# Down projection of an MLP by Strassen's seven products on two token blocks

## The chip, the cores and the metric

The kernel runs on one core of a Trainium2 chip. The metric is the device time of one execution in microseconds; the median of several runs is compared.

## The reference

One layer of a streaming encoder for 384 tokens, 256 of a new stream and 128 of eight running ones. A mixer (pooling branch, Mamba-2 branch, gates) comes first, then the MLP, which is what the change touches. Width 2048, hidden width 8192, all in float32:

```python
def layer(x, st_pool, st_conv, st_ssm, pos0, p):
    m, new_pool, new_conv, new_ssm = mixer(rmsnorm(x, p['g_mix_pre']), ...)
    x = x + rmsnorm(m, p['g_mix_post'])
    hdn = jnp.square(jax.nn.relu(rmsnorm(x, p['g_mlp_pre']) @ p['w_up'])) @ p['w_down']
    x = x + rmsnorm(hdn, p['g_mlp_post'])
    return x, new_pool, new_conv, new_ssm
```

## The kernel before

The 384 tokens are three blocks of 128. Every matrix product is made of three matmuls on split operands: each float32 operand is cut into a high part (`fp32r`, cast by ScalarE, line 71) and a low part (the rest, by VectorE, line 73), and high x high, high x low and low x high are accumulated in PSUM. Weights come from DRAM as tiles of 128 x 1024 through SyncE's queue (`wfetch`, line 61), are split by `wsplit` (line 66) and rotate through three buffers each for the raw tile, its high and its low part. PSUM is two pools of four banks, `mmtile` and `sstile`.

The mixer takes about the first 1800 us. Then comes the MLP, lines 730 to 803. `x1` (the residual, 3 x 2048 per partition) is transposed and split into `x1h`, `x1l`, the moving operands of the up projection (lines 718 to 727), and its norm factor `r2` is computed beside it. The loop over `c8` takes eight chunks of 1024 hidden rows. In each chunk:

- Up: eight tiles `f8` of 128 hidden rows, each 2 weight tiles x 8 k x 3 matmuls with 384 moving columns (the tokens). The result is scaled, rectified, squared (`ht`), and split into `hh` and `hl`, which have the hidden rows on the partitions.
- Down: four blocks `nb` of 512 output columns. For each, `moving` (line 638) walks four weight tiles of two k each; for each k and each token block `b` three matmuls (lines 648 to 650) with the tokens stationary and 512 weight columns moving. After the last k, VectorE adds the PSUM tile into `hacc` in SBUF (line 778; in the first chunk ScalarE copies it, line 776).

After the last chunk's blocks come the square sums, the gain `gpo2`, the norm and the residual, and the output is stored (lines 781 to 795). A scheduler sets the order of instructions on each engine. The lines that matter in the loop:

```python
for c8 in range(NC):
    hh = []
    for f8 in range(8):
        ...
        hh.append((h, l))
    for nb in range(4):
        o = [mmtile(f"wd{c8}_{nb}_{b}") for b in range(3)]
        ...
        moving(o, [(io["w_down"][c8, nb, kp], ...) for kp in range(4)], hh, ..., done)
```

Of the kernel before, what the change touches and what calls it, by code (L numbers as in the profile page):

```python
# [14 lines left out]
P = 128  # L15
T = 384
TP = 256
NB = 8
TS_ = 16
DM = 2048  # L20
# [14 lines left out]
def build(ctx, tc, io):  # L35
    nc = tc.nc
    v, s, te, gp, sy = nc.vector, nc.scalar, nc.tensor, nc.gpsimd, nc.sync
# [5 lines left out]
    dram = ctx.enter_context(tc.tile_pool(name="dram", bufs=1, space=DRAM))  # L43
# [6 lines left out]
    def mmtile(name):  # L50
        return psm.tile([P, 512], F32, tag="mm", name=name)
# [4 lines left out]
    hold = [None, None]  # L56
# [19 lines left out]
    def wload(src, name):  # L76
        return wsplit(wfetch(src, name))
# [94 lines left out]
    w = wpool.tile([P, 1024], F32, tag="w", name="w_p0_0")  # L172
# [465 lines left out]
    x1 = res.tile([P, 3, DM], F32, name="x1")  # L638
    r2 = res.tile([P, T], F32, name="r2")

    def moving(o, units, lhs, tail, done):
        nk = len(lhs)

        def mm(b, wh, wl, k, k2):
            t = slice(b * P, b * P + P)
            c = slice(k2 * 512, k2 * 512 + 512)
            mh, ml = lhs[k][0][:, t], lhs[k][1][:, t]
            te.matmul(o[b], mh, wh[:, c], start=k == 0, stop=False)  # L648
            te.matmul(o[b], mh, wl[:, c], start=False, stop=False)  # L649
            te.matmul(o[b], ml, wh[:, c], start=False, stop=k == nk - 1)  # L650

        n = len(units)
        for kp in range(n - tail):
            wh, wl = wload(*units[kp])
            for k2 in range(2):
                for b in range(3):
                    mm(b, wh, wl, kp * 2 + k2, k2)
        w = [wload(*units[kp]) for kp in range(n - tail, n)]
        for b in range(3):
            for i, (wh, wl) in enumerate(w):  # L660
                for k2 in range(2):
                    mm(b, wh, wl, (n - tail + i) * 2 + k2, k2)
            done(b)
# [19 lines left out]
    with tc.tile_pool(name="phf", bufs=1, side="right", reuse_waits="tile") as pf, tc.tile_pool(  # L683
# [5 lines left out]
        for nb in range(4):  # L689
# [13 lines left out]
        for i in range(4):  # L703
# [9 lines left out]
                )  # L713
            if i == 0:
                gate[1] = ins
    pga = ctx.enter_context(tc.tile_pool(name="pga", bufs=1, reuse_waits="tile"))
    xs2 = []
    for k in range(KD):
        tr = sstile(f"trm{k}")
# [5 lines left out]
        s.activation(h, tr[:, :T], AF.Copy, scale=g1)  # L725
        v.scalar_tensor_tensor(out=l, in0=tr[:, :T], scalar=g1, in1=h.bitcast(F32), op0=ALU.mult, op1=ALU.subtract)
        xs2.append((h, l))
    mpool.close()

    with tc.tile_pool(name="phg", bufs=1, reuse_waits="tile") as pg, tc.tile_pool(  # L730
        name="phg2", bufs=2, reuse_waits="tile"
    ) as pg2:
        st = pg.tile([P, 3, 4], F32, name="st2")
        for b in range(3):
            for i in range(4):
                q = pg2.tile([P, 512], F32, tag="q3", name=f"q2_{b}_{i}")
                s.activation(q, x1[:, b, blk(i)], AF.Square, accum_out=st[:, b, i : i + 1])
        dg = pg.tile([P, 3, P], F32, name="dg2")
        for b in range(3):
            y = postnorm(pg2, st, b, "n2")  # L740
# [4 lines left out]
        hacc = pg.tile([P, 3, DM], F32, name="hacc")  # L745
        gpo = pg.tile([P, DM], F32, name="gpo2")
        gp.dma_start(gpo, io["g_mlp_post"].partition_broadcast(P))
        st3 = pg.tile([P, 3, 4], F32, name="st3")
        NC = 8
        for c8 in range(NC):  # L750
            hh = []
            for f8 in range(8):
                f = c8 * 8 + f8
                if f == 0:
                    ps = mmtile("pj_up0")[:, :T]
                    half(ps, 0, wload(io["w_up"][0, 0], "up0_0"), xs2)
                    hold[:] = gate
                    half(ps, 1, wload(io["w_up"][0, 1], "up0_1"), xs2)
                else:
                    ps = proj([io["w_up"][f, 0], io["w_up"][f, 1]], xs2, f"up{f}")  # L760
                    hold[:] = [None, None]
                t = pg2.tile([P, T], F32, tag="t", name=f"ht{f}")
                v.scalar_tensor_tensor(out=t, in0=ps, scalar=0.0, in1=r2, op0=ALU.max, op1=ALU.mult)
                s.activation(t, t, AF.Square)
                h = pg2.tile([P, T], F32R, tag=f"hh{f8}", name=f"hh{f}", bufs=1)
                l = pg2.tile([P, T], F32R, tag=f"hl{f8}", name=f"hl{f}", bufs=1)
                s.activation(h, t, AF.Copy)
                v.tensor_tensor(l, t, h.bitcast(F32), ALU.subtract)
                hh.append((h, l))
            for nb in range(4):  # L770
                o = [mmtile(f"wd{c8}_{nb}_{b}") for b in range(3)]

                def done(b):
                    dst = hacc[:, b, blk(nb)]
                    if c8 == 0:
                        s.copy(dst, o[b])
                        return
                    v.tensor_tensor(dst, o[b], dst, ALU.add)
                    if c8 < NC - 1:
                        return  # L780
                    q = pg2.tile([P, 512], F32, tag="q3", name=f"q3_{nb}_{b}")
                    s.activation(q, dst, AF.Square, accum_out=st3[:, b, nb : nb + 1])
                    v.tensor_tensor(dst, dst, gpo[:, blk(nb)], ALU.mult)
                    if nb < 3:
                        return
                    y = postnorm(pg2, st3, b, "n3")
                    for i in range(4):
                        z = hacc[:, b, blk(i)]
                        xb = x1[:, b, blk(i)]
                        if i >= (0, 2, 3)[b]:  # L790
                            s.activation(z, z, AF.Copy, scale=y)
                            gp.tensor_tensor(z, z, xb, ALU.add)
                        else:
                            v.scalar_tensor_tensor(out=z, in0=z, scalar=y, in1=xb, op0=ALU.mult, op1=ALU.add)
                        sy.dma_start(io["y"][b][:, blk(i)], z)

                moving(
                    o,
                    [(io["w_down"][c8, nb, kp], f"wd{c8}_{nb}_{kp}") for kp in range(4)],
                    hh,  # L800
                    3 if c8 == NC - 1 and nb == 3 else 0,
                    done,
                )


def _consts(np):
# [29 lines left out]
def _moving(np, w):  # L836
    r, c = w.shape
    return np.ascontiguousarray(w.reshape(r // 256, 2, P, c // 512, 512).transpose(3, 0, 2, 1, 4)).reshape(c // 512, r // 256, P, 1024)


# [79 lines left out]
```

## Time and profile before

| | |
|---|---|
| Median of 3 runs | 2888.16 us (2887.67 to 2889.95) |
| Span of the profiled execution | 2886.1 us |
| TensorE busy | 2862.9 us (99%) |
| VectorE busy | 1548.9 us (54%) |
| ScalarE busy | 1108.4 us (38%) |
| GpSimd busy | 142.4 us (5%) |
| Moved by the DMA engines | 448.82 MB, 156 GB/s on the mean |

The profile is of one execution, whose own time is not listed beside its span; the three timed runs lie 1.6 to 3.9 us above the span, the median 2.1. PE is TensorE's matmuls, PEld its weight loads, DVE VectorE, ACT ScalarE, POOL GpSimd, SP SyncE. A group of instructions is a line such as "L650 PE MATMUL wd<-wh_wd,hl 128*128 128x512 f32 x768 | 298.9, 389 | 0.0": line 650, engine, operation, output and inputs, shape, count; then busy time in us, the mean of one in ns, and the idle time before them in us with what ended it. In a timeline the first number is the start and the second the duration, in us, and what stands in brackets is the idle time before. A window's row has for each engine its busy time and count in that stretch, then the granted TensorE clock (1 is full speed), the mean busy share of the 16 DMA engines, and GB/s. The rows of DMA issues give the size of one and the median time from issue to landing; queue q1 carries what SyncE issues, q0 what GpSimd issues.

### The profile page before, as it was taken

Reading aid. Unit: us, or ns where it says so; the run is one execution under the profiler, and the core shown is the slowest. Engines: PE = TensorE matmul, PEld = TensorE weight load, DVE = VectorE, ACT = ScalarE, POOL = GpSimd, SP = SyncE. Lnnn points to the kernel's source line nnn. Section 1 sums busy time; section 2 is a strip of 40 time slices with the busy share of each in tenths; the row PEclk is TensorE's granted clock in tenths of the full one; section 3 lists DMA queues with packets and bytes.
Section 4 is the critical chain, followed back from the end, with each engine's and each line's share of the span. In section 5 each row is a group of like instructions: output and inputs, shape, how many; then the busy total and the mean of one; then the engine's idle time right before and its main releaser. Section 6 shows DMA issues by size and latency. Waiting matters only on the chain.

```text
span 2886.1 us, 40192 instructions
## 1 busy us (share of the span) xinstructions
PE 2862.9 (99%) x16165; PEld 2702.5 (94%) x16165; DVE 1548.9 (54%) x2306; ACT 1108.4 (38%) x1628; POOL 142.4 (5%) x178
## 2 busy tenths in 40 slices
PE   9999999999999999999999999999999999999998
PEld 8999999999999999999999988989898998989896
DVE  7773335668678678677533334534444444444445
ACT  5343224445445345344422223533232333333233
POOL 0000000011011011011000000000000000000001
PEclk9999999999999999999999999999999999999999
DMA  6444445466456456466744453434443444444443
GB/s 214 132 130 140 137 137 190 149 200 211 160 196 211 151 203 210 146 221 204 224 147 152 146 179 120 130 126 130 126 130 126 130 126 131 125 131 124 131 125 117
DMA packets 141914, 448.82 MB, mean 156 GB/s; under 512 B 17456, under 2 KB 41072, under 8 KB 137120
## 3 DMA queue, kind: packets, MB, share of 16 engines
q1 hardware_dynamic: 133152, 410.14, 44.9%
q0 software_dynamic: 8576, 36.13, 3.3%
q8 instruction: 126, 2.06, 0.3%
q14 instruction: 60, 0.49, 0.1%
HBM read 404.48 MB, written 41.72 MB: 155 GB/s over the span
## 4 chain that ended last, share of the span: by engine, by line
PE 98%; DVE 1%; DMA 0%; ACT 0%; issue 0%; SPq 0%; DVEq 0%; ACTq 0%
PE pj_up L82 6%; PE pj_up L81 6%; PE pj_up L80 6%; PE wd L650 6%; PE wd L649 6%; PE wd L648 6%; PE pj_x L82 5%; PE pj_x L80 5%; PE pj_x L81 5%; PE pj_z L81 3%; PE pj_z L82 3%; PE pj_z L80 3%; PE pj_sp L80 3%; PE pj_sp L82 3%; PE pj_sp L81 3%; PE pj_gb L80 2%
## 5 line engine op out<-in xcount | busy, mean ns | idle before, releaser
L81 PE MATMUL pj_up<-x1l,wh_up 128*128 128x384 f32 x1024 | 343.2, 335 | 0.0
L80 PE MATMUL pj_up<-x1h,wh_up 128*128 128x384 f32 x1024 | 343.1, 335 | 0.0
L82 PE MATMUL pj_up<-x1h,wl_up 128*128 128x384 f32 x1024 | 342.7, 335 | 0.0
L650 PE MATMUL wd<-wh_wd,hl 128*128 128x512 f32 x768 | 298.9, 389 | 0.0
L649 PE MATMUL wd<-wl_wd,hh 128*128 128x512 f32 x768 | 298.9, 389 | 0.0
L648 PE MATMUL wd<-wh_wd,hh 128*128 128x512 f32 x768 | 298.7, 389 | 0.0
L73 DVE TENSOR_TENSOR wl_wd<-w_wd,wh_wd 128x1024 fp32r<-128x1024 f32 x128 | 156.9, 1225 | 263.2 <-ACT wh_wd L71 263.2
L71 ACT ACTIVATE wh_wd<-w_wd 128x1024 fp32r<-128x1024 f32 x128 | 136.1, 1063 | 350.9 <-PE wd L650 284.3
L80 PE MATMUL pj_x<-xgh,wh_x 128*128 128x384 f32 x768 | 264.0, 344 | 0.0
L73 DVE TENSOR_TENSOR wl_up<-w_up,wh_up 128x1024 fp32r<-128x1024 f32 x128 | 156.9, 1226 | 198.1 <-ACT wh_up L71 198.1
L82 PE MATMUL pj_x<-xgh,wl_x 128*128 128x384 f32 x768 | 261.0, 340 | 0.0
L71 ACT ACTIVATE wh_up<-w_up 128x1024 fp32r<-128x1024 f32 x128 | 135.9, 1064 | 325.6 <-PE pj_up L81 264.8
L81 PE MATMUL pj_x<-xgl,wh_x 128*128 128x384 f32 x768 | 259.8, 338 | 0.0
L80 PEld LDWEIGHTS pj_up<-x1h,wh_up 128*128 128x128 f32 x1024 | 192.5, 188 | 0.7 <-ACT x1h L725 0.4
L81 PEld LDWEIGHTS pj_up<-x1l,wh_up 128*128 128x128 f32 x1024 | 192.6, 188 | 0.4
L82 PEld LDWEIGHTS pj_up<-x1h,wl_up 128*128 128x128 f32 x1024 | 192.5, 188 | 0.1
L81 PE MATMUL pj_z<-xgl,wh_z 128*128 128x384 f32 x512 | 173.1, 338 | 0.0
L80 PE MATMUL pj_z<-xgh,wh_z 128*128 128x384 f32 x512 | 172.9, 338 | 0.0
L82 PE MATMUL pj_z<-xgh,wl_z 128*128 128x384 f32 x512 | 172.9, 338 | 0.0
L650 PEld LDWEIGHTS wd<-wh_wd,hl 128*128 128x128 f32 x768 | 144.1, 188 | 30.0
L649 PEld LDWEIGHTS wd<-wl_wd,hh 128*128 128x128 f32 x768 | 144.1, 188 | 29.9
L648 PEld LDWEIGHTS wd<-wh_wd,hh 128*128 128x128 f32 x768 | 144.2, 188 | 29.6
(280 smaller groups left out, 6230.9 us busy)
## 6 DMA issues: line engine op xcount, KB each, us to landing
w_up<-w_up SPq DMA_DIRECT2D x128, 512.0 KB, 3.4
w_wd<-w_down SPq DMA_DIRECT2D x128, 512.0 KB, 3.4
w_x<-w_in SPq DMA_DIRECT2D x96, 512.0 KB, 3.7
w_z<-w_in SPq DMA_DIRECT2D x64, 512.0 KB, 3.5
w_sp<-w_ssd SPq DMA_DIRECT2D x64, 512.0 KB, 3.5
w_ga<-w_in SPq DMA_DIRECT2D x32, 512.0 KB, 3.5
w_pp<-w_pp SPq DMA_DIRECT2D x32, 512.0 KB, 3.5
hs<-ssm SPq DMA_DIRECT2D x16, 1024.0 KB, 6.3
```

The lines of the kernel that those rows point to most:

```text
L71: s.activation(h, w, AF.Copy)
L73: v.tensor_tensor(l, w, h.bitcast(F32), ALU.subtract)
L80: te.matmul(out, wh, xh, start=first, stop=False)
L81: te.matmul(out, wh, xl, start=False, stop=False)
L82: return te.matmul(out, wl, xh, start=False, stop=last)
L648: te.matmul(o[b], mh, wh[:, c], start=k == 0, stop=False)
L649: te.matmul(o[b], mh, wl[:, c], start=False, stop=False)
L650: te.matmul(o[b], ml, wh[:, c], start=False, stop=k == nk - 1)
```

## The change

In the first seven chunks the down product of token blocks 0 and 1 is made by Strassen's scheme (Winograd's form) on 2 x 2 blocks. The token operand is cut into blocks 0 and 1 by k-halves (k-tiles 0 to 3 and 4 to 7 of the chunk); the weights into k-halves by column halves of 512 out of a group of 1024 columns (two passes `p` a chunk). Seven products of 128 tokens x 512 rows x 512 columns take the place of eight. Token block 2 keeps its plain product and shares the weights' splits (results 7 and 8).

- Weights: the four blocks 11, 12, 22, 21 of a pass are loaded as raw tiles of 128 x 2048 (five buffers). The sums 11+12 and 12+22 are made by a transfer that GpSimd issues and that adds the DRAM block into the raw tile (`add_far`); the sums 22+(11+12) and 21+(22+11+12) by VectorE in place (`add`). Each of the eight steps of a pass splits its 2048 columns anew, two units of 1024 each.
- Tokens: four sums of token blocks are made a chunk by VectorE and split (`token_sums`); `t8` keeps the unsplit hidden tiles.
- Results: nine PSUM tiles a pass are copied to SBUF by ScalarE (`ev`, three buffers) and stored (first chunk) or added (later) into DRAM (`acc_scr`) by transfers that GpSimd issues. In the last chunk they are read back, and seven VectorE operations a pass form the outputs of blocks 0 and 1 from the seven products (`merge`).
- The last chunk's down product is as it was, from its own weight array, added to the merged results, then the final norm.
- `x1` is stored to DRAM after the mixer and its SBUF room given to the MLP; it is read back, and `gpo2` loaded, in the last chunk.
- The order in the MLP is written out by hand (`run`): loads are issued up to eight units ahead, splits four units ahead, with a fourth pair of split buffers (`xh`, `xl`).

The diff, cut to its core:

```diff
+    gp.dma_start(x1_scr, x1)
+    mpool.close()
+    pga_hold = ExitStack()
...
+    def split4(w, name):
+        turn[0] += 1
+        if turn[0] % DEPTH:
+            return wsplit((w, name))
+        h = pg.tile([P, 1024], F32R, tag="xh", name=f"wh_{name}")
+        l = pg.tile([P, 1024], F32R, tag="xl", name=f"wl_{name}")
+        s.activation(h, w, AF.Copy)
+        v.tensor_tensor(l, w, h.bitcast(F32), ALU.subtract)
+        return h, l
+
+    def run(units, far=8):
...
+        for i in range(far):
+            fetch(i)
+        for i in range(DEPTH):
+            prep(i)
+        for i, (_, _, mm, post, soon) in enumerate(units):
+            fetch(i + far)
+            mm(hl[i])
+            if soon:
+                post()
+            prep(i + DEPTH)
+            if not soon:
+                post()
...
+    def token_sums(k):
+        a11, a12 = t8[:, k, :P], t8[:, 4 + k.start : 4 + k.stop, :P]
+        a21, a22 = t8[:, k, P:TP], t8[:, 4 + k.start : 4 + k.stop, P:TP]
+        f = [sf[:, i, k, :] for i in range(4)]
+        v.tensor_tensor(f[0], a22, a21, ALU.subtract)
...
+        s.activation(sh[:, :, k, :], sf[:, :, k, :], AF.Copy)
+        v.tensor_tensor(sl[:, :, k, :], sf[:, :, k, :], sh[:, :, k, :].bitcast(F32), ALU.subtract)
...
+        def add(d, n):
+            v.tensor_tensor(raw[d], raw[d], raw[n], ALU.add)
+
+        def add_far(d, n):
+            gp.dma_start(raw[d], src[n], accum_op=ALU.add)
+
+        steps = [
+            ("11", True, [(0, tok(0, 0)), (7, tok(0, 2))], lambda: add_far("11", "12")),
+            ("12", True, [(8, tok(0, 2))], lambda: add_far("12", "22")),
+            ("21", True, [(1, tok(4, 0)), (7, tok(4, 2))], nothing),
+            ("22", True, [(2, sums(3)), (8, tok(4, 2))], nothing),
+            ("11", False, [(4, sums(0))], lambda: add("22", "11")),
+            ("12", False, [(6, sums(2))], lambda: add("21", "22")),
+            ("22", False, [(5, sums(1))], nothing),
+            ("21", False, [(3, tok(4, 1))], nothing),
+        ]
...
+        def evict(r, o):
+            e = pg.tile([P, 512], F32, tag="ev", name=f"ev{nm}_{r}", bufs=3)
+            s.copy(e, o)
+            if c8 == 0:
+                gp.dma_start(acc_scr[p][r], e)
+            else:
+                gp.dma_start(acc_scr[p][r], e, accum_op=ALU.add)
...
+                def prep(_, j=j, q=q, kd=kd, hc=half_cols, then=then):
+                    hl = split4(raw[kd][:, hc], f"wd{nm}_{j}_{q}")
+                    if q:
+                        then()
+                    return hl
...
+    def merge(p):
+        a1, a2, a3, a4, a5, a6, a7 = ac[p][:7]
+        v.tensor_tensor(a2, a1, a2, ALU.add)
...
+    for i in range(NC - 1):
+        hh = [] if i else hh0
+        units += up_units(i, hh, 0 if i else 1, lambda f8: token_sums(slice(0, 3)) if f8 == 6 else None)
+        for p in range(2):
+            units += down_units(i, p, hh)
+    hh = []
+    units += up_units(c8, hh, 0, after_last)
+    units += last_units(hh)
+    with tc.manual_schedule():
+        run(units)
```

In a pass the letters before `True` or `False` name the raw tile of the step (and whether it is loaded for it), the list its products (result number and token operand), and the last entry what is started once the tile's second half is split.

More of the change, by code (lines that the diff above doesn't have):

```diff
@@ L715, in build @@
                 gate[1] = ins
-    pga = ctx.enter_context(tc.tile_pool(name="pga", bufs=1, reuse_waits="tile"))
+    gp.dma_start(x1_scr, x1)
+    mpool.close()
+    pga_hold = ExitStack()
+    pga = pga_hold.enter_context(tc.tile_pool(name="pga", bufs=1, side="right", reuse_waits="tile"))
     xs2 = []
@@ L744, in build @@
         s.copy(r2, bc[:, :T])
[L745 to L758, printed above, removed]
-                else:
[L760 to L776, printed above, removed]
-                        return
[L778 to L802, printed above, removed]
-                )
@@ new lines, in run, with fetch, prep @@
+    def run(units, far=8):
+        n = len(units)
+        got, hl = [None] * n, [None] * n
+        def fetch(i):
+            if i < n and units[i][0]:
+                got[i] = units[i][0]()
+        def prep(i):
+            if i < n:
+                hl[i] = units[i][1](got[i])
+        for i in range(far):
[10 more added lines that the diff above has]
+                post()
+            hl[i] = got[i] = None
@@ new lines, in up_evict, with up_units, mm, post @@
+    def up_evict(f, ps):
+        f8 = f % 8
+        t = t8[:, f8, :]
+        v.scalar_tensor_tensor(out=t, in0=ps, scalar=0.0, in1=r2, op0=ALU.max, op1=ALU.mult)
+        s.activation(t, t, AF.Square)
+        h = pg.tile([P, T], F32R, tag=f"hh{f8}", name=f"hh{f}")
+        l = pg.tile([P, T], F32R, tag=f"hl{f8}", name=f"hl{f}")
+        s.activation(h, t, AF.Copy)
+        v.tensor_tensor(l, t, h.bitcast(F32), ALU.subtract)
+        return h, l
+    def up_units(c8, hh, skip=0, after=nothing):
+        out = []
+        for f8 in range(skip, 8):
+            f = c8 * 8 + f8
+            ps = []
+            for q in range(2):
+                def mm(hl, f=f, q=q, ps=ps):
+                    if q == 0:
+                        ps.append(mmtile(f"pj_up{f}")[:, :T])
+                    half(ps[0], q, hl, xs2)
+                def post(f=f, f8=f8, q=q, ps=ps):
+                    if q:
+                        hh.append(up_evict(f, ps[0]))
+                        after(f8)
+                out.append(
+                    (lambda f=f, q=q: wfetch(io["w_up"][f, q], f"up{f}_{q}"), lambda w: split4(*w), mm, post, True)
+                )
+        return out
@@ new lines, in build @@
+    hh0 = []
+    ps = mmtile("pj_up0")[:, :T]
+    half(ps, 0, wload(io["w_up"][0, 0], "up0_0"), xs2)
+    hold[:] = gate
+    half(ps, 1, wload(io["w_up"][0, 1], "up0_1"), xs2)
+    hold[:] = [None, None]
+    hh0.append(up_evict(0, ps))
+    units = []
+    for i in range(NC - 1):
+        hh = [] if i else hh0
+        units += up_units(i, hh, 0 if i else 1, lambda f8: token_sums(slice(0, 3)) if f8 == 6 else None)
+        for p in range(2):
+            units += down_units(i, p, hh)
+    hh = []
```

178 lines of the change are left out of this document (166 added, 12 removed).

## The prediction

> **What bounds the kernel now.** I read the head of the profile page first, then the chain that ended last, then the timeline of the matmuls.
>
> ```profile
> span 2886.1 us, 40192 instructions
> PE 2862.9 (99%) x16165; PEld 2702.5 (94%) x16165; DVE 1548.9 (54%) x2306; ACT 1108.4 (38%) x1628; POOL 142.4 (5%) x178
> PE 98%; DVE 1%; DMA 0%; ACT 0%; issue 0%; SPq 0%; DVEq 0%; ACTq 0%
> ```
>
> TensorE is busy for 99% of the span and carries 98% of the chain, so a matmul that is no longer issued shortens the end, as long as nothing else becomes late. What one matmul is worth must come from the timeline, not from the group's mean:
>
> ```profile
> L650 PE MATMUL wd<-wh_wd,hl 128*128 128x512 f32 x768 | 298.9, 389 | 0.0
> 1899.90 0.39 PE L648 MATMUL wd<-wh_wd,hh 128*128 128x512 f32 x1
> ...
> 1900.58 0.39 PE L648 MATMUL wd<-wh_wd,hh 128*128 128x512 f32 x1
> 1900.81 0.39 PE L649 MATMUL wd<-wl_wd,hh 128*128 128x512 f32 x1
> 1999.67 0.33 PE L82 MATMUL pj_up<-x1h,wl_up 128*128 128x384 f32 x1
> ...
> 2001.23 0.33 PE L82 MATMUL pj_up<-x1h,wl_up 128*128 128x384 f32 x1
> ```
>
> The mean is 389 ns, but starts at 1899.90 and 1900.58 are three matmuls apart: 0.227 us each. The records overlap; 389 ns is how long one is in the pipe. In the up projection nine starts take 1.56 us, 0.173 us each. All 2304 down matmuls are therefore worth 2304 x 0.227 = 523 us of the span, not 896.
>
> **What is removed.** A chunk of 1024 hidden rows had 8 k-tiles x 4 column blocks x 3 token blocks x 3 matmuls = 288. Now a pass over one half of the output columns has eight steps with 2, 1, 2, 2, 1, 1, 1, 1 products, 11 in all, each 4 k-tiles x 3 matmuls: 132 for a pass, 264 for a chunk. Seven chunks change, the eighth stays: 7 x 24 = 168 matmuls less, 168 x 0.227 = **-38.1 us**. Stationary and moving shapes stay as they were, so I keep the spacing.
>
> **Splitting the weights.** Each step needs its own high and low part of 2048 weight columns: 16 splits of 1024 columns a pass, where a chunk had 16 and now has 32. The prices:
>
> ```profile
> L73 DVE TENSOR_TENSOR wl_wd<-w_wd,wh_wd 128x1024 fp32r<-128x1024 f32 x128 | 156.9, 1225 | 263.2 <-ACT wh_wd L71 263.2
> L71 ACT ACTIVATE wh_wd<-w_wd 128x1024 fp32r<-128x1024 f32 x128 | 136.1, 1063 | 350.9 <-PE wd L650 284.3
> L573 DVE TENSOR_TENSOR hs<-hs,decb 128x2048 f32<-128x2048 f32 x16 | 36.5, 2284 | 0.0
> L776 ACT COPY hacc<-wd 128x512 f32<-128x512 f32 x12 | 7.0, 587 | 7.4 <-PE wd L650 6.6
> 1825.16 2.02 ACT L71 ACTIVATE wh_up<-w_up 128x1024 fp32r<-128x1024 f32 x2
> 1817.58 1.22 DVE L73 TENSOR_TENSOR wl_up<-w_up,wh_up 128x1024 fp32r<-128x1024 f32 x1
> 1818.71 1.66 DVE L726 SCALAR_TENSOR_TENSOR x1l<-trm,vec,x1h 128x384 fp32r<-128x384 f32 x3
> ```
>
> A pass lasts 132 x 0.227 = 29.9 us on TensorE. VectorE has in it 16 x 1.225 + 2 weight sums x 2.28 = 24.2 us; ScalarE 16 x 1.063 + 9 copies out of PSUM x 0.587 = 22.3 us. Both fit on the mean. Not everywhere, though. A unit (half a step) is 2.72 us with two products, but 1.36 us with one, and the last eight units are short: 10.9 us. Back to back, a split costs ScalarE 1.01 us (two in 2.02) and VectorE 1.13 us (1817.58 to 1818.71). In those 10.9 us ScalarE has eight splits and about five copies, 8.1 + 2.9 = 11.0; VectorE 9.0. ScalarE is just full. Four split buffers keep three units ready, 4.1 us of cover, against 2.3 us for one split through both engines, so I lose only the excess and some waits at the turns: between 0 and 2 us a pass, taken 0.5, the row being so near balance: 14 x 0.5 = **+7 us**.
>
> **Token sums** (five small VectorE sums, one split, a chunk) run beside up units of 24 x 0.173 = 4.2 us, whose splits take 2.3; their last quarter follows the first step and is due two steps later: 0. The DVE adds of results into `hacc` (0.69 us each) go; VectorE was not the bound, so they give nothing back.
>
> **Accumulating transfers, the unknown.** No transfer of before adds. Per chunk GpSimd now issues four weight sums of 1 MB (into SBUF) and 18 results of 256 KB (into DRAM; in the first chunk plain stores), 8.5 MB, beside 16 MB of loads. Nearest rows:
>
> ```profile
> q1 hardware_dynamic: 133152, 410.14, 44.9%
> q0 software_dynamic: 8576, 36.13, 3.3%
> hs<-ssm SPq DMA_DIRECT2D x16, 1024.0 KB, 6.3
> new_ssm_s<-hs POOLq DMA_DIRECT2D x16, 1024.0 KB, 4.8
> new_ssm_p<-pe POOLq DMA_DIRECT2D x32, 64.0 KB, 2.5
> L561 POOL DMA_DIRECT2D new_ssm_p<-pe x32 | 17.5, 546 | 423.1 <-ACT E L493 406.8 <-ACT pe L560 11.9 <-ACT E L505 4.4
> ```
>
> Queue q1 moved 410 MB in 44.9% of 2886 us, 0.32 MB/us while busy; q0 36.1 MB in 3.3%, 0.38 MB/us. An issue costs GpSimd 0.55 us, and a small store lands after 2.5 us, so about 2 us are fixed. Low end: an accumulate costs what a store does, 2.8 us of the queue for 1 MB, 4.8 to landing. High end: it also reads its destination and costs twice or three times, 5.5 to 8.3 us of the queue. I take 1.5 times, since reads may overlap writes.
>
> Where is it due? The second pass is the tighter one: its predecessor is 29.9 us of short units, while the first pass follows 67 us of up projection. Call its start T. The sum 11+12 is issued once unit 1's split is done, at about T - 0.3; 12+22 after unit 3's, T + 2.5. They are needed before PE reaches unit 8 (T + 19.0) and unit 10 (T + 21.8), less 2.3 us for the split. So from T - 0.3 to T + 19.4 queue q0 must move two sums and one result between them, 2.36 MB: 17 us after the fixed 2.5. Alone: 6.2 us at a store's cost, 9.3 at 1.5, 12.4 at double. But the last weight tile of the pass and the first three of the next up stage, 2.6 MB or more, load at the same time; if the queues share evenly it is 12, 19 and 25 us, if the 8 KB rows of a sum get more than the 4 KB rows of a load, nearer 9, 13 and 17. At 1.5 times that is in time or 2 us late, seven times: 0 to 14, taken **+5 us**, since three units of cover lie behind it. What waits behind a late sum: ScalarE's split of that unit, and in its queue the copies out of PSUM and all later splits; on GpSimd nothing, because it only issues. The three `ev` buffers make a copy wait for the result three before it: 8.2 us apart in short units against 2.5 to 6 us to land, so 0 while the queue keeps up.
>
> The Trainium skill, "Collectives: The Full Stack", section "The bandwidth ceiling: the fold count and why AG ≠ RS ≠ AR", speaks against this change: a reduce in the DMA reads two sources through the same ring and got 32.35 against 62.28 GB/s. No run shown here tells; by that factor, 1.93, my even-sharing case would be 7 us late in each second pass.
>
> **Entry and end.** `x1` is stored (3 MB) and its room reused; the first write there, the first up tile's eviction, may wait. 3 MB at 0.38 is 8.3 us, and the first up tile needs about as long, with four PSUM tiles of cover: 0 to 3, taken **+1**. `x1` and the gain come back during the last down stage, 288 x 0.227 = 65 us ahead of their use: 0. The last chunk and the final normalisation do what they did.
>
> **Sum.** 2886.1 - 38.1 + 7 + 5 + 1 = 2861 on the profiled span; the median of the timed runs, 2888.16, lies 2.1 above that span, so **2863 us**.
>
> **Rivals.**
> *A, slower: the sums land late.* If an accumulate costs double and the queues share evenly, unit 10 waits 25 - 17 = 8 us in each of seven second passes, 56 us. Gaps like that also cost clock. The row of the one gap in the old MLP:
>
> ```profile
> 1808.01 1.11 PE L721 MATMUL trm<-cst,x 128*128 128x128 f32 x4 [3.18 <-DVE x L711]
> 1806.00:1822.00 16.00, 13.60 (x75) 12.25 (x76) 14.24 (x27) 14.07 (x33) 1.96 (x3) 0.79 0.30 106
> ```
>
> After 3.18 us idle the granted clock is 0.79 over 16 us, 16 x 0.21 = 3.4 us lost; seven times 24. With 5 of it already in the sum: 2863 + 56 + 24 - 5 = **2938**, from 2894 at a delay of 5 us to 2990 at three times the cost. It decides from about 1.7 times a store's cost with even sharing. For it: two reads where a copy has one. Against: on the mean, 16.8 MB / 0.32 + 8.9 MB x 2 / 0.38 = 99 us of queue in a chunk of 127; only the burst is too dense.
> *B, almost nothing: the splits set the pace.* If each short stretch loses 2 us instead of 0.5, by waits between ScalarE, VectorE and TensorE at every unit, 14 x 2 = 28: **2884**. ScalarE's 11.0 of 10.9 us speaks for it, the 4.1 us of cover against.
> *C, a larger gain:* 168 x 389 ns = 65 us, **2835**, if duration counted. The starts exclude it.
> That fewer matmuls are not issued after all is excluded by the loops' counts.
>
> **How the numbers follow.** About 0.2% (5.8 us) can be told from no change. My forecast, 2848 to 2876, gets 0.58; B 0.10, of which a fifth is faster and the rest within 0.2%; A 0.31; C 0.01. Faster 0.61, same 0.08, slower 0.31. The forecast's low end is the sum with no loss, 2850, the high end its terms' upper ends. The range goes from 2848 to 2940: forecast, B, and half of A, leaving out about 0.17. The likeliest case's own range is 2848 to 2876.
>
> **What would show it.** Right: matmul records fewer by 168, starts 0.227 us apart, down stages of about 60 us, a sum landing in under 10 us, no idle row of TensorE over 1 us in units 8 to 11 of the second pass. Wrong: ScalarE waiting on the DMA of a raw tile, TensorE on `wh_wd` with the clock below 1 (A); TensorE waiting a little on VectorE at every short unit with the sums landed early (B).

## The result, and the profile after

The changed kernel takes 2894.3 us (median; 2891.5 to 2896.6), the one before 2888.2 (2887.4 to 2889.9): a ratio of 1.0020, 95% interval 1.0012 to 1.0028. It is 6 us slower; the prediction was 2863. The profiled execution took 2891.45 us, 1.75 more than its span, and is the fastest of these runs, so the traces differ by only 3.6 us of span.

From the page of the changed kernel (busy time by engine, GpSimd's DMA queue, the chain's shares) and its view of DMA issues (count, size, median us from issue to landing):

```profile
span 2889.7 us, 40652 instructions
PE 2837.1 (98%) x15997; PEld 2671.2 (92%) x15997; DVE 1741.1 (60%) x2472; ACT 1283.8 (44%) x1868; POOL 280.3 (10%) x352
q0 software_dynamic: 31328, 109.54, 15.8%
PE 82%; issue 7%; DMA 6%; DVE 3%; POOL 1%; ACT 1%; SPq 0%; POOLq 0%; DVEq 0%; ACTq 0%
```

```profile
acc_scr<-ev POOLq DMA_DIRECT2D x126, 256.0 KB, 7.1
raw<-w_down POOLq DMA_DIRECT2D x28, 1024.0 KB, 9.5
```

There are 168 matmuls fewer, as counted. But TensorE carries 82% of the chain, where it had 98%; DMA has 6% where it had 0. Queue q0 moved three times the bytes of before (109.54 against 36.13 MB) in almost five times the share (15.8% against 3.3%).

The second chunk's down stage, from the matmul timeline of the changed kernel, first matmul of the stage and first of the next up stage:

```profile
2011.33 0.39 PE L911 MATMUL wd<-wh_wd,hh 128*128 128x512 f32 x1
...
2078.16 0.34 PE L80 MATMUL pj_up<-x1h,wh_up 128*128 128x384 f32 x1
```

It lasts 66.8 us; 264 matmuls at 0.227 are 59.9. Adding up whatever a start-to-start exceeds 0.227, the seven changed stages lose 1.4, 6.9, 6.3, 5.6, 5.0, 5.9 and 5.8 us, 36.9 in all: nearly the whole of the 38.1 that was saved. The first is the chunk whose results are stored and not added. The up stages lose nothing. In each of the other six chunks the loss sits at the same four places: unit 12 of the first pass (0.35), and in the second pass units 0 (1.2 to 2.4), 10 (1.8 to 2.4) and 12 (1.7).

That second pass in the timelines, ScalarE, then TensorE and VectorE (start, duration, in brackets the idle time before and what ended it):

```profile
2031.54 0.57 ACT L875 COPY ev<-wd 128x512 f32<-128x512 f32 x1
...
2041.34 0.59 ACT L875 COPY ev<-wd 128x512 f32<-128x512 f32 x1 [4.07 <-DMA acc_scr<-ev]
...
2065.49 0.59 ACT L875 COPY ev<-t 128x512 f32<-128x512 f32 x1 [5.98 <-DMA acc_scr<-ev]
```

```profile
2042.94 0.50 PE L911 MATMUL wd<-wh_wd,hh 128*128 128x512 f32 x1 [1.12 <-ACT wh_wd L71]
...
2067.08 0.50 PE L911 MATMUL wd<-wh_wd,sh 128*128 128x512 f32 x1 [1.05 <-ACT wh_wd L71]
...
2072.81 0.50 PE L912 MATMUL wd<-wl_wd,sh 128*128 128x512 f32 x1 [1.47 <-DVE wl_wd L73]
```

```profile
2069.34 2.29 DVE L856 TENSOR_TENSOR raw<-raw,raw 128x2048 f32<-128x2048 f32 x1
```

At 2037.3 ScalarE wanted to copy a result and all three `ev` buffers were still on their way to DRAM. It stood 4.07 us; behind that copy in its queue was the split for the second pass's unit 0, and TensorE waited for it. At 2059.5 the same again for 5.98 us, ahead of unit 10's split. After each wait VectorE has two splits to catch up and, at 2069.34, a weight sum of 2.29 us ahead of the split of unit 12: the third place.

What GpSimd had issued, and how long its transfers took to land in that stage (results of line 879, then weight sums of line 859, each with its minimum, median and maximum):

```profile
2032.40 1.73 POOL L879 DMA_DIRECT2D acc_scr<-ev  x2 [3.65 <-ACT ev L875]
...
2045.57 0.86 POOL L859 DMA_DIRECT2D raw<-w_down  x1 [2.50 <-DVE wl_wd L770]
...
2048.20 0.87 POOL L859 DMA_DIRECT2D raw<-w_down  x1 [0.88 <-DVE wl_wd L73]
2048.74 1.21 POOL L879 DMA_DIRECT2D acc_scr<-ev  x1
```

```profile
DMA to landing us min/median/max: 3.8/7.2/16.7
```

```profile
DMA to landing us min/median/max: 7.8/9.5/15.9
```

The result copied at 2031.54 and issued at 2032.40 landed at 2041.26; its buffer was wanted at 2037.27. The sum issued at 2048.20 landed after 15.9 us, and the result issued right behind it on the same queue after 16.7, at 2065.46; the copy ran at 2065.49. So it is in all six chunks: what is waited for last before unit 10 is a copy's buffer, held by the result behind the second sum; the sum itself lands 1.3 us before it here (2064.12). The first sum is issued at 2045.57, 2.6 us behind the pass's first matmul, because the split that it follows stood behind the held copy.

Why so long is seen in the windows (the last three numbers are granted TensorE clock, mean busy share of the 16 DMA engines, GB/s; the share adds up the times of the packets, so it can pass 1), first of the changed kernel's second pass and of its whole down stage, then of a whole down stage of before:

```profile
2041.30:2051.30 10.00, 8.12 (x35) 6.18 (x34) 6.41 (x6) 8.10 (x11) 4.36 (x5) 1.00 1.08 328
2051.30:2061.30 10.00, 10.00 (x45) 8.28 (x45) 6.74 (x6) 4.67 (x5) 1.71 (x2) 1.00 1.04 231
2011.33:2078.16 66.83, 61.58 (x266) 49.25 (x265) 49.93 (x45) 42.12 (x53) 17.99 (x21) 1.00 0.91 196
```

```profile
2013.00:2079.00 66.00, 66.00 (x297) 55.05 (x296) 27.22 (x28) 17.95 (x18) 0.00 (x0) 1.00 0.42 128
```

The DMA engines, busy 42% of the old stage, are busy 91% of the new one and full for these 20 us. In the second ten they move only 231 GB/s at a full share. The clock stays at 1.00 in this trace. Of those 20 us, the two queues' rows in the view of DMA (packets, MB, share):

```profile
q0 software_dynamic: 725, 2.78, 69.5%
q1 hardware_dynamic: 772, 2.78, 36.0%
```

Both moved the same bytes, but GpSimd's queue, with the adding transfers, kept the engines busy almost twice as long for them.

Last, the end, in the timelines of the changed kernel and of before (TensorE's last matmul, VectorE's first sums of the norm, GpSimd's residual addition):

```profile
2868.40 5.45 POOL L982 TENSOR_TENSOR ac<-ac,x1b 128x512 f32<-128x512 f32 x4 [60.62 <-ACT ac L981]
...
2871.31 0.39 PE L1000 MATMUL wd<-wh_wd,hl 128*128 128x512 f32 x1
...
2871.41 1.23 DVE L672 TENSOR_TENSOR n_n<-st 128x1 f32<-128x1 f32 x1
```

```profile
2859.63 0.29 DVE L670 TENSOR_TENSOR n_n<-n_n,st 128x1 f32<-128x1 f32 x3
...
2871.98 0.39 PE L650 MATMUL wd<-wh_wd,hl 128*128 128x512 f32 x1
```

From the last matmul's start to the end it is 2889.7 - 2871.3 = 18.4 us; before, 2886.1 - 2872.0 = 14.1 (by the unrounded times 4.2 us more). Before, the scheduler had put the norm's first sums ahead (2859.63); in the order written by hand they run after the last block, and beside GpSimd's additions one of 128 elements takes 1.23 us.

### The profile page after: what moved, and what is told of

It reads as the page before. It is cut to its first block, busy times and chain, and to the rows that moved or that the text cites. A ratio compares the mean times of both kernels' runs of the same rounds, so it can differ in the third digit from the quotient of the medians.

```text
span 2889.7 us, 40652 instructions
## 1 busy us (share of the span) xinstructions
PE 2837.1 (98%) x15997; PEld 2671.2 (92%) x15997; DVE 1741.1 (60%) x2472; ACT 1283.8 (44%) x1868; POOL 280.3 (10%) x352
## 3 DMA queue, kind: packets, MB, share of 16 engines
q0 software_dynamic: 31328, 109.54, 15.8%
## 4 chain that ended last, share of the span: by engine, by line
PE 82%; issue 7%; DMA 6%; DVE 3%; POOL 1%; ACT 1%; SPq 0%; POOLq 0%; DVEq 0%; ACTq 0%
PE pj_up L81 5%; PE pj_up L80 5%; PE pj_up L82 5%; PE pj_x L82 5%; PE pj_x L80 5%; PE pj_x L81 5%; DMA acc_scr<-ev 4%; PE pj_z L81 3%; PE pj_z L82 3%; PE pj_z L80 3%; PE pj_sp L80 3%; PE pj_sp L81 3%; PE pj_sp L82 3%; PE pj_gb L80 2%; PE pj_gb L81 2%
## 5 line engine op out<-in xcount | busy, mean ns | idle before, releaser
L73 DVE TENSOR_TENSOR wl_wd<-raw,wh_wd 128x1024 fp32r<-128x1024 f32 x168 | 201.2, 1222 | 88.2 <-ACT wh_wd L71 83.0
L71 ACT ACTIVATE wh_wd<-raw 128x1024 fp32r<-128x1024 f32 x168 | 172.9, 1057 | 52.4 <-DMA raw<-w_down 21.0
L81 PE MATMUL pj_sp<-abl,wh_sp 128*128 128x384 f32 x512 | 171.0, 334 | 0.0
L80 PE MATMUL pj_sp<-abh,wh_sp 128*128 128x384 f32 x512 | 171.0, 334 | 0.0
L82 PE MATMUL pj_sp<-abh,wl_sp 128*128 128x384 f32 x512 | 171.0, 334 | 0.0
L73 DVE TENSOR_TENSOR wl_up<-w_up,wh_up 128x1024 fp32r<-128x1024 f32 x97 | 118.7, 1225 | 85.5 <-ACT wh_up L71 85.5
L73 DVE TENSOR_TENSOR wl_sp<-w_sp,wh_sp 128x1024 fp32r<-128x1024 f32 x64 | 78.4, 1224 | 119.8 <-ACT wh_sp L71 119.5
L80 PEld LDWEIGHTS pj_x<-xgh,wh_x 128*128 128x128 f32 x768 | 144.4, 188 | 2.5 <-issue 1.4
L82 PEld LDWEIGHTS pj_x<-xgh,wl_x 128*128 128x128 f32 x768 | 144.2, 188 | 2.6 <-issue 2.6
L81 PEld LDWEIGHTS pj_x<-xgl,wh_x 128*128 128x128 f32 x768 | 144.3, 188 | 1.1 <-issue 0.2
```

Of the source, the lines that this page charges most:

```text
L71: s.activation(h, w, AF.Copy)
L73: v.tensor_tensor(l, w, h.bitcast(F32), ALU.subtract)
L80: te.matmul(out, wh, xh, start=first, stop=False)
L81: te.matmul(out, wh, xl, start=False, stop=False)
L82: return te.matmul(out, wl, xh, start=False, stop=last)
```

## The experiments

Three theories of the 36.9 us lost: **Q**, results that land late hold the three copy buffers and so ScalarE; **S**, the two weight sums made by transfers land late; **V**, VectorE's own weight sums and splits are too slow for the short units. Ratios are to the kernel before, run on the same chip; over the chips used it took 2888.1 to 2888.8 us, so times are also compared with the changed kernel's 2894.3 directly.

### prices: each transfer alone

Behind the end of the changed kernel, on empty queues, each waiting for the one before:

```diff
+        gp.dma_start(big, wd[0, 0, 0])
+        gp.dma_start(big, wd[0, 0, 1])
+        for i in range(3):
+            gp.dma_start(big, wd[1, 0, i], accum_op=ALU.add)
+        for i in range(3):
+            gp.dma_start(small, tail["x1"][:, 1, :512])
+        for i in range(3):
+            gp.dma_start(small, tail["x1"][:, 1, :512], accum_op=ALU.add)
```

> At the end of the kernel, with the queues empty, GpSimd issues one after the other, each waiting for the one before: two plain loads of 1 MB, three adding loads of 1 MB into the same tile, three plain stores of 256 KB into one DRAM tile, three adding stores of 256 KB into the same. From the rows of before a plain 1 MB takes about 5 us from issue to landing and 256 KB about 2.6. If adding costs as much as copying (low end of the prediction): 5 and 2.6. At 1.5 times, as taken: 6.4 and 2.9. At double: 7.7 and 3.3; at three times 10.5 and 4. The time is longer by the sum, 40 to 75 us, and says nothing else.

The plain 1 MB loads landed after 6.2 and 5.1 us. By line (issue time on GpSimd in ns, then landing): adding 1 MB, plain 256 KB (the first of three stood behind the 1 MB), adding 256 KB:

```profile
L1057 POOL DMA_DIRECT2D x1b<-w_down x3: 860/873/889, 2898.5 to 2915.3; - x3
...
DMA to landing us min/median/max: 7.9/8.1/8.1
```

```profile
L1059 POOL DMA_DIRECT2D acc_scr<-x1b x3: 542/570/904, 2915.8 to 2926.7; - x3
...
DMA to landing us min/median/max: 2.3/2.3/8.0
```

```profile
L1061 POOL DMA_DIRECT2D acc_scr<-x1b x3: 855/876/890, 2929.3 to 2938.1; - x3
...
DMA to landing us min/median/max: 4.0/4.1/4.2
```

Alone, adding costs a result 4.1 instead of 2.3 us and a sum 8.1 instead of 5 to 6, with 0.87 instead of 0.57 us of GpSimd for an issue. By the expectation's scale that is about double for a sum and three times for a result. In the second chunk's first pass the sums land as they do alone (7.8 and 8.3 us); the 10.8 and 15.9 of its second pass, and the results' median of 7.1, are longer, and the rest is company. (The one timed execution took 2949.0 us, longer by the added transfers.)

### plain_results: results stored, never added

```diff
-            if c8 == 0:
-                gp.dma_start(acc_scr[p][r], e)
-            else:
-                gp.dma_start(acc_scr[p][r], e, accum_op=ALU.add)
+            gp.dma_start(acc_scr[p][r], e)
```

> The nine results of a pass are stored plainly in every chunk, not added in DRAM (the sum over chunks is left out; what is read back is the last chunk's part). In the profile of the changed kernel the first chunk, which stores plainly, loses 1.4 us in its down stage and the six that add lose 5.0 to 6.9 us. Theory Q (the adding result transfers land so late that ScalarE waits for one of the three copy buffers, and the splits behind it come late): all seven lose 1.4, 6 x 4.5 = 27 us less, a time of about 2867 us. Theory S (the 1 MB sums of weights are what is late; the results only share their queue): the 2 us at the second pass's unit 10 stay in each of six chunks, about 2880 us.

2865.9 us (2864.5 to 2869.7), ratio 0.9922 (0.9907 to 0.9937), what Q expected. Unit 0 of the second pass loses nothing in any chunk, unit 10 only 0.8 in two of them; unit 12 keeps 0.35 to 1.7. Copies still wait for the result behind the second sum (14 to 16 us to landing), but this comes early enough for unit 10.

### no_far_sums: no weight sums by transfer

```diff
         def add_far(d, n):
-            gp.dma_start(raw[d], src[n], accum_op=ALU.add)
+            pass
```

> The two adding transfers of weights a pass are left out (steps 5 and 6 then use the raw blocks; the products are not the right ones). Theory Q: the stall at the second pass's first unit (1.2 to 2.4 us) stays, since no sum is in the queue when the first pass's results go out; that at unit 10 (1.8 to 2.4 us) goes: 6 x 2.1 = 13 us less, about 2881 us. Theory S: both go, 6 x 3.9 = 23 us less, about 2871 us. Third theory V (VectorE's own adds of weights make unit 12 late): the 1.7 us at unit 12 stay under both.

2869.0 us (2868.8 to 2869.9), ratio 0.9932 (0.9917 to 0.9946): in time it is S that fits. The places decide more finely: unit 0 keeps its 1.3 to 1.7, which is Q's alone; unit 10 is gone; unit 12 is down to 0.35. So Q and S both hold. Each removal alone gives back 25 to 28 us of 37, because both load the same DMA engines: their busy share over the second chunk's down stage is 0.91 with both, 0.72 in `plain_results`, 0.66 here, and 0.42 with neither.

What adding costs those engines follows from queue q0 in the pages of three runs: this one, the last, and `nothing_late` below, which has neither kind of adding transfer (packets, MB, share of 16 engines' span; above each its span):

```profile
span 2865.2 us, 40652 instructions
q0 software_dynamic: 24416, 109.54, 12.3%
```

```profile
span 2867.4 us, 40528 instructions
q0 software_dynamic: 27296, 80.18, 11.3%
```

```profile
span 2853.3 us, 40514 instructions
q0 software_dynamic: 20384, 80.18, 7.2%
```

The queue is busy 0.123 x 2865 = 352 us with sums, 0.113 x 2867 = 324 with adding results, and 205 with neither. The 28 sums cost 147 us, 5.2 each; at the 0.38 MB/us of plain transfers 1 MB is 2.8, so the factor is 1.9. The 108 results cost 119 us more for adding, 1.1 each on top of 0.69: 2.6 times. The packets show that an adding result also goes out in smaller pieces: 27296 - 20384 = 6912, 64 more for each of the 108. And the median time to landing of a result, from the same three runs' DMA issues, is 4.3 us (plain, beside sums), 5.5 (adding, no sums) and 2.8 (plain, no sums). With both it was 7.1: adding costs a result 2.7 or 2.8 us, the sums on its queue 1.5 or 1.6.

### no_vector_adds: VectorE's two weight sums left out

```diff
         def add(d, n):
-            v.tensor_tensor(raw[d], raw[d], raw[n], ALU.add)
+            pass
```

> VectorE's two adds of 2048 weight columns a pass (2.28 us each) are left out (the last products are not the right ones). Theory V: the stalls at unit 12, 0.36 us in the first pass and 1.0 to 1.7 in the second, go: 7 x 2 = 14 us less, about 2880 us. If unit 12 is late only because ScalarE was held up before, by Q, no more than 3 us change: 2891 us or more. The stalls at units 0 and 10 stay under both.

2887.6 us (2885.7 to 2890.2), ratio 0.9997 (0.9987 to 1.0006), about 7 us below the changed kernel and between the two expectations. Chunk 0, where nothing is added in DRAM, loses 0 instead of 1.4. Chunks 1 to 6 still lose 4.1 to 6.3: of the 1.7 at unit 12 of the second pass at most 0.35 is left, but 0.35 to 0.7 stay at unit 12 of the first, and in five of the six units 10 and 11 lose 3.5 to 4.3 instead of about 2. There the granted clock falls to half for about 3.4 us behind unit 10's wait, first in this window of the second chunk (in the 3.4 us behind it it is 1.00 again):

```profile
2066.70:2070.00 3.30, 3.30 (x8) 2.61 (x9) 2.79 (x3) 3.30 (x5) 1.91 (x3) 0.50 0.89 115
```

The chunk whose clock stays at 1.00 loses 4.1. So VectorE's sums cost the 0.35 where nothing else is late and the 1.7 at unit 12 behind late sums; part of what leaving them out gives is taken back by the clock.

The profiled execution of the changed kernel, the fastest of 14, has no such fall in these stages. The trace of `prices`, the same code up to its last transfers, has one behind unit 10 in four of its six later chunks:

```profile
2068.90:2072.20 3.30, 3.27 (x8) 2.60 (x9) 3.30 (x3) 3.00 (x5) 1.72 (x3) 0.50 0.94 110
```

Units 10 and 11 lose 3.8 to 4.8 there and unit 12 0.2 to 0.6 instead of 1.7, so that stages lose 5.6 to 7.2 with it and 5.5 and 5.9 without. Whether it is what makes the other 13 timed executions up to 5 us slower than the profiled one is open.

### nothing_late: all three left out

Results stored, no sums by transfer, none by VectorE (the three edits above together).

> Edit: results are stored instead of added in all chunks, both adding weight transfers of a pass and both of VectorE's weight sums are left out, so the output lacks the sums over chunks and the weight sums. All matmuls, splits, copies and loads of the changed kernel stay. It measures what 168 matmuls less are worth when none of the new work is late. Theory M (a matmul is worth its spacing of 0.227 us, and the splits and copies of ScalarE fit into the short units): the 36.9 us that TensorE loses in the seven changed chunks of the changed kernel go, 2894 - 37 = 2857, or from the kernel with plain results (2866, 12.7 lost) 2866 - 12.7 = 2853; so 2853 to 2857, every changed down stage 59.9 to 60.3 us. Rival R (ScalarE's eight splits and five copies in the last eight units, 11.0 of 10.9 us, cost by themselves what the prediction put on them): 0.5 us a pass more, 7 in all: 2860 to 2864, down stages 60.9, with TensorE waiting on ScalarE's split in units 10 to 15.

2854.1 us (2853.9 to 2855.1), ratio 0.9883 (0.9868 to 0.9898): theory M. The same down stage in its timeline, and ten microseconds of its second pass in the windows:

```profile
2010.85 0.39 PE L908 MATMUL wd<-wh_wd,hh 128*128 128x512 f32 x1
...
2070.70 0.34 PE L80 MATMUL pj_up<-x1h,wh_up 128*128 128x384 f32 x1
```

```profile
2050.90:2060.90 10.00, 10.00 (x46) 8.29 (x45) 4.24 (x4) 5.03 (x6) 1.07 (x2) 1.00 0.13 52
```

59.85 us, with no gap in any of the seven changed stages: 32 splits and 18 copies a chunk fit into ScalarE, short units included. The DMA engines are busy 13% in these ten, where the changed kernel has 104%, and 42% of the whole stage, where it has 91%. The whole kernel gains 34.0 us, its trace 32.8 of span: the stages' 38.1, less an end that is 4.8 us longer in this trace and a first down stage that begins 0.9 later.

### four_copy_buffers

Room for a fourth `ev` buffer comes from `sf`, whose last quarter reuses the first's room.

```diff
-    sf = pg.tile([P, 4, 4, P], F32, name="sf")
+    sf = pg.tile([P, 4, 3, P], F32, name="sf")
...
-            e = pg.tile([P, 512], F32, tag="ev", name=f"ev{nm}_{r}", bufs=3)
+            e = pg.tile([P, 512], F32, tag="ev", name=f"ev{nm}_{r}", bufs=4)
```

> Four copy buffers for results instead of three (the unsplit token sums get three quarters of their room). Theory Q: a copy then waits for the result four before it. By the landings in the profile of the changed kernel the copy that waited 4.07 us at the end of the first pass would find its buffer free, and the one that waited 5.98 us in the second pass too. So the stall at the second pass's first unit goes (6 x 1.75 = 10 us), that at unit 10 shrinks to what the late sum itself costs (0 to 2 us): 2874 to 2885 us, about 2879. Theory S (late sums and a full queue, not the buffers, hold ScalarE): under 4 us change, 2890 us or more.

2883.4 us (2881.3 to 2885.1), ratio 0.9980 (0.9970 to 0.9989). Unit 0 is free. The waits, of the changed kernel and of this one (in total, times, longest):

```profile
ACT ev L875 <- DMA acc_scr<-ev: 59.1, 19, 6.0
...
ACT wh_wd L71 <- DMA raw<-w_down: 21.0, 7, 3.3
```

```profile
ACT wh_wd L71 <- DMA raw<-w_down: 56.0, 14, 5.7
...
ACT ev L876 <- DMA acc_scr<-ev: 3.1, 6, 0.9
```

ScalarE no longer waits for a buffer but for the sums, which land no sooner. The fourth buffer is worth 11 us; units 10 to 12 still lose 3.7 to 4.5 us a chunk (with a clock fall in three of the six).

### sums_on_vector: the sums by VectorE instead of by transfer

```diff
         def add_far(d, n):
-            gp.dma_start(raw[d], src[n], accum_op=ALU.add)
+            v.tensor_tensor(raw[d], raw[d], raw[n], ALU.add)
```

> The sums 11+12 and 12+22 are made by VectorE in place too, from the raw tiles; no transfer adds weights. The queue is as free as in the run without these sums (2869 us). VectorE gets two more adds of 2.28 us a pass: 16 x 1.13 + 4 x 2.2 = 27 of 29.9 us, and they fall into the short units of the pass before, which hold 9.0 of 10.9 us already: 13.5 of 10.9, less up to 4 us of cover. Theory V (VectorE's place in short units is the dear thing): 1 to 3 us lost a pass, 2880 to 2905 us, about 2890, with TensorE waiting on the low parts around units 10 to 14. If the cover takes it: 2869 to 2874 us.

2904.5 us (2900.7 to 2905.2), ratio 1.0050 (1.0035 to 1.0065), at the upper edge of what was expected. VectorE and TensorE in its timeline:

```profile
2023.41 2.29 DVE L859 TENSOR_TENSOR raw<-raw,raw 128x2048 f32<-128x2048 f32 x1
```

```profile
2026.90 0.50 PE L912 MATMUL wd<-wl_wd,hh 128*128 128x512 f32 x1 [1.81 <-DVE wl_wd L73]
```

The sum now stands ahead of a split that a unit of 1.36 us waits for, in both passes: 6.0 to 9.1 us a chunk (with a clock fall behind unit 4 of the first pass in three of the seven). VectorE's 60% over the span left room on the mean, not there.

### tail_order: the norm's first sums ahead again

The three small operations of each token block that need only the first three column blocks run before the last block, as they did.

```diff
+        if nb == 2:
+            tail["pre"] = [prenorm(lp2, st3, b, "n3") for b in range(3)]
...
-            y = postnorm(lp2, st3, b, "n3")
+            y = postnorm(lp2, st3, b, "n3", tail["pre"][b])
```

> The first three VectorE instructions of the last norm (the sum of three block sums, scaled) are issued after the third column block instead of behind the last one; the scheduler had put them there before. In the profile of the changed kernel the work after the last matmul ends 3.6 us later than before. Theory tail (hand order): the end comes 2 to 3 us earlier, about 2892 us, and the stretch from the last matmul to the end of the span goes from 17.9 to about 15 us; the down stages lose what they lost. If the later end is due to another cause (the residual's late return, the stores), the stretch stays at 17 to 18 us.

```profile
2861.83 0.15 DVE L672 TENSOR_TENSOR n_n<-st 128x1 f32<-128x1 f32 x1
```

2890.5 us (2888.8 to 2892.9), ratio 1.0005 (0.9996 to 1.0015), some 4 us less than the changed kernel. From the last matmul to the end it is 15.2 us instead of 18.4. 1.0 us of the longer end stays, all after VectorE's last instruction; what it is, is open.

### two_stage_results and two_stage_four_buffers: add where nothing waits

The down stage only stores its results, to a second place (`st_scr`); the next up stage, where the DMA engines were 41% busy before, adds them from DRAM to DRAM, three in each of six tiles `f8`. The merges come two tiles `f8` later. The order of `tail_order` is in it.

```diff
+            gp.dma_start((acc_scr if c8 == 0 else st_scr)[p][r], e)
...
+            if i > 1 and f8 < 6:
+                for n in range(f8 * 3, f8 * 3 + 3):
+                    gp.dma_start(acc_scr[n // 9][n % 9], st_scr[n // 9][n % 9], accum_op=ALU.add, max_dma_last_dim=512)
```

> Results are stored plainly into a second DRAM area in each chunk, and added from there into the accumulators by 18 DRAM-to-DRAM adding transfers of 256 KB beside the next chunk's up projection, where the queues have room; the last chunk's are added on reading back. With the last norm's order as in the run for the tail. Theory Q: down stages as in the run with plain results (2866 us), the end 2.5 us earlier: about 2863 us (2859 to 2868). Against it: 18 transfers at about 2.3 us of the queue each are 41 us of the 54 us before the first sum of the chunk is issued; if they spread, the first pass's sums come late, 2 to 5 us a chunk: 2875 to 2895 us.

2862.9 us (2861.8 to 2864.4), ratio 0.9909 (0.9894 to 0.9924). Its DMA issues:

```profile
st_scr<-ev POOLq DMA_DIRECT2D x108, 256.0 KB, 4.4
acc_scr<-st_scr POOLq DMA_DIRECT2D x90, 256.0 KB, 16.8
```

An adding transfer takes 16.8 us here, and only the next one of its kind waits for it. The window of the up stage behind the second chunk's down stage:

```profile
2073.40:2139.90 66.50, 66.50 (x385) 66.50 (x384) 30.58 (x37) 25.32 (x32) 19.13 (x19) 1.00 1.09 261
```

The DMA engines are as full there as in the changed kernel's second pass, yet TensorE is busy throughout: in this kernel full DMA engines cost time only where something waits for them. What stays is 1.6 to 2.6 us a chunk, nearly all in unit 12. The second variant adds the fourth copy buffer:

> Edit: the kernel whose results are stored in the down stage and added from DRAM to DRAM in the next up stage, with the final norm's first sums ahead again, now with four copy buffers instead of three. Theory Q (the copy buffers mattered only because an adding transfer of a result landed after 7 us or more; plain stores land after 4.4 us, so three are enough): no change, 2861 to 2864 as with three, losses of TensorE 1.5 to 2.6 us a chunk in unit 12. Rival C (the copies still wait for their buffers in the short units and cost unit 12 its 1.2 to 1.7 us): 7 x 1.4 = 10 us faster, 2853.

2856.8 us (2855.8 to 2857.6), ratio 0.9891 (0.9875 to 0.9908): 31 us faster than the kernel before. Q expected no change and was wrong, C's direction was right, for 6 of its 10 us. In the first variant's waits the copies still show:

```profile
ACT ev L881 <- DMA st_scr<-ev: 23.5, 7, 4.2
```

That is, but for one of 1.7 us, one wait in each changed chunk (the first chunk's copies go to `acc_scr` and are not in this row): the result issued right behind the second sum lands with it, after 14 to 16 us, however cheap its own transfer is. A fourth buffer takes just that wait away; 0.7 to 1.6 us a chunk remain.

## Why the prediction was wrong

By its own terms, in us, with what the traces gave:

| term | predicted | measured |
|---|---|---|
| 168 matmuls | -38.1 | -38.1 (`nothing_late`: stages of 59.85) |
| splits in the short units | +7 | 0 from splits and copies; 4.9 from VectorE's sums (14 x 0.35) |
| late sums | +5 | 12.6 at unit 10 of the second pass, 9.0 at unit 12 beyond the 0.35, shared with the next row |
| copies waiting for `ev` | 0 | 10.5 at unit 0 of the second pass, and part of the row above |
| entry | +1 | 0, the first up stage lasts 74.4 in both traces |
| end | 0 | +4.2 |

The sum is -38.1 + 4.9 + 32.1 + 4.2 = +3.1; the spans differ by 3.6. That 4.9 lies near the 7 is luck: the splits and copies, for which the 7 was put in, cost nothing.

**The step that failed** is the accumulating transfers and what waits for them, at three points.

First the zero on the copies: "8.2 us apart in short units against 2.5 to 6 us to land, so 0 while the queue keeps up". Both numbers were off. Results are copied in pairs, so at the end of the first pass the buffer was wanted 5.7 us after its copy began (2031.54 to 2037.27), and it landed 8.9 after its issue, in other places after 11 and 16.7. The argument costed the queue for the sums with the results in it, and the results with the sums left out.

Second the price: "I take 1.5 times, since reads may overlap writes". In time of the engines it was 1.9 for the sums and 2.6 for the results. The factor of 1.93 that the prediction took from two rates of the Trainium skill ("Collectives: The Full Stack", section "The bandwidth ceiling: the fold count and why AG ≠ RS ≠ AR") and cited against the change agrees with the sums' 1.9; no run here shows its own case, a collective. The prediction set the load against a chunk ("99 us of queue in a chunk of 127"), but GpSimd's queue moves nearly all of its part, 8.36 MB in the second chunk, in the down stage. An estimate by stage, from the numbers of that sentence: 8.9 x 2 / 0.38 = 47 us of adding transfers and, with half of the loads, 8.4 / 0.32 = 26, together 73 in a stage of 60.

Third the size of the lateness. The second sum was needed at T + 19.4, T being the start of the second pass's first matmul in each trace. Over the chunks from the second on it lands at T + 16.8 to 19.3 with plain results, at T + 21.3 to 22.2 with adding results and four buffers, and at T + 20.6 to 21.3 in the changed kernel, where the held copy delays the first sum's issue from T + 0.6 to T + 2.6. So the "2 us late" of the prediction came (2.1 on the mean, in six chunks). It allowed 14 us for that and took 5, "since three units of cover lie behind it". The cover took nothing of it, and the 9.0 at unit 12, VectorE's sum ahead of the next split, had no term.

**Rival A** had the factor about right (double) and its consequence too large: it made unit 10 wait 8 us, 56 in all, and the clock fall for another 24. Unit 10 waited 2.1 on the mean: the queues shared evenly in bytes, not in time (69.5% to 36.0%), so the sums got through sooner than at half of the engines. The clock stayed at 1.00 in the profiled execution; where it fell (`prices`), it was at half for 3.4 us, and the stages lost hardly more. **Rival B**'s 2884 came nearer than my number, with its symptom (TensorE waiting on VectorE at a short unit) at unit 12; but its cause, the splits, is refuted by `nothing_late`, where ScalarE's "11.0 of 10.9" costs nothing. **C** is excluded by the 59.85.

**The end** was put at "did what they did". The instructions did; the order did not, because the scheduler's placing of the norm's sums was lost with the order written by hand. That is a part of the change I read and did not cost.

**Right** were the spacing as the worth of a matmul, the second pass as the tighter one with unit 10 in it, token sums and up stages at nothing, and the sign named for the slower case: ScalarE waiting on the DMA of a raw tile. My high end, 2940, held the result; the forecast did not.

## What to carry to other kernels

Set the time that a new transfer takes the DMA engines against what they have free in the stage where it runs, not in a whole chunk: these engines were 42% busy in the down stage before and 91% after, full for 20 us of it, and then everything on the queue became late together, down to a 256 KB store behind a 1 MB sum. Whatever waits for such a transfer (here three copy buffers, and behind them ScalarE's splits) inherits the delay, so it needs buffers for the longest landing, or the transfer belongs in a stage where nothing waits for it, even if it fills the engines there. And when an order is written out by hand, list what the scheduler had moved ahead.

## What the runs showed of the hardware that I had not expected

- An adding transfer takes the DMA engines 1.9 times (1 MB into SBUF) to 2.6 times (256 KB into DRAM) as long as a plain one; alone it lands after 8.1 instead of 5 to 6 us, and 4.1 instead of 2.3.
- A small transfer behind a large one on GpSimd's queue lands with it: 16.7 us for an adding 256 KB (4.1 alone), 15.4 for a plain one (`two_stage_results`; 2.3 alone).
- A two-input VectorE operation on 128 x 1 elements took 1.23 us beside a two-input addition on GpSimd, 0.15 without it; it ended with that addition (both at 2872.6).
- With the engines full, the two queues moved equal bytes (2.78 MB each in 20 us), although a byte of the one cost almost twice the time of the other.
- Behind TensorE's wait at unit 10 the granted clock fell to half for about 3.4 us in some chunks and not in others of the same code (`prices`: four of six; the changed kernel's profile: none of six).
